# Moving a sum over 128 partitions from TensorE to GpSimd, and product P6 of one block behind P1 of the next

## The chip, the cores and the metric

One Trainium2 chip (trn2), one core. The metric is the device time of one execution in microseconds (us); a kernel is described by the median of its runs. Every run also has a profiled span, from the first recorded instruction to the last.

Names: TensorE (PE, its weight loads PEld), VectorE (DVE), ScalarE (ACT), GpSimd (POOL), SyncE (SP).

## The reference

```
x: (16, 256, 512), w1: (512, 4096), w2: (2048, 512), all float32
h = x @ w1
gate, value = split(h, 2)
h = maximum(gate, 0) * value
out = h @ w2
```

## The kernel before

The kernel works in float16 with float32 accumulation and replaces blocks of eight half-size products by seven products of sums (P1 to P7). Each of four stretches of 1024 rows goes through sixteen blocks of hidden columns (two plain ones at the very start) and then through the second matrix. Because sums in float16 can overflow or lose digits, squares of the inputs are collected in a tile `st` (128 x 152); at the end all entries must lie between two bounds. That is the verdict: VectorE counts the good entries of each partition, the 128 counts are added up, and a flag tells every engine whether to run a slow "general way", which is not taken here.

A block of seven products shares three PSUM tiles, X, Y and W, between TensorE (adds a product) and ScalarE or VectorE (reads what is there so far):

```python
def P1(self):                                   # TensorE -> X, then ScalarE copies X to Y
    self.X = psx.tile([P, TH], F32, name="X", tag="X")
    self.mm("P1", self.X, True)
    self.Y = psy.tile([P, TH], F32, name="Y", tag="Y")
    nc.scalar.copy(out=self.Y, in_=self.X)
def P5(self):                                   # TensorE -> W, ScalarE reads W into pu
    ...
    nc.scalar.activation(self.p5, self.W, COPY, scale=GS)
def P6(self):                                   # TensorE adds to Y, ScalarE reads Y into pu
    self.mm("P6", self.Y, False)
    nc.scalar.activation(self.u2, self.Y, COPY, scale=GS)
def P7(self):                                   # TensorE adds to Y again: only after that reading
    self.mm("P7", self.Y, False)
    nc.vector.scalar_tensor_tensor(out=self.c22, in0=self.Y, scalar=GS, in1=self.p5, op0=MULT, op1=ADD)
    ...
# ... cut: P2, P3, P4
```

P5, P6, P7 and P4 need weight sums T1 to T4, which GpSimd makes (`w_T<-w_stage`). Block 2 is the first of the seven-product kind, and its order is written by hand:

```python
for at, n in ((1, "P2"), (2, "P5"), (6, "P3")):
    plan[NPLAIN * PERIOD + at] = NPLAIN, n
plan[NPLAIN * PERIOD + 5] = NPLAIN + 1, "P1"
```

So TensorE runs P5, P6, P1 of block 3, P3, P5 of block 3, P7. The verdict at the end:

```python
def judge():                                    # VectorE: good entries of each partition
    # ... cut
    nc.vector.tensor_reduce(out=fit[:, :1], in_=ok, axis=mybir.AxisListType.X, op=ADD)
def count(fit):                                 # TensorE: sum over partitions, against a column of ones
    n = P * st.shape[1]
    ps = psx.tile([P, TH], F32, name="X", tag="X")
    nc.tensor.matmul(ps[:1, :1], fit[:, :1], fit[:, 1:], start=True, stop=True)
    nc.vector.tensor_scalar(out=flag, in0=ps[:1, :1], scalar1=n - 0.5, scalar2=None, op0=LT)
```

Of the kernel before, what the change touches and what calls it, by code (L numbers as in the profile page):

```python
# [9 lines left out]
F32, F32R, F16 = dt.float32, dt.float32r, dt.float16  # L10
ADD, SUB = mybir.AluOpType.add, mybir.AluOpType.subtract
MAX, MULT = mybir.AluOpType.max, mybir.AluOpType.mult
LE, GE, LT, ABS_MAX = (getattr(mybir.AluOpType, n) for n in ("is_le", "is_ge", "is_lt", "abs_max"))
# [3 lines left out]
P = 128  # L17
TH = 512
PERIOD = 7
NWARM = 24  # L20
NPLAIN = 2
# [5 lines left out]
@with_exitstack  # L27
def kernel(ctx: ExitStack, tc: tile.TileContext, x, w1, w2, out):






    nc = tc.nc
    x2 = x.flatten_outer_dims()
    out2 = out.flatten_outer_dims()
    flagpool = ctx.enter_context(tc.tile_pool(name="flagpool", bufs=1))
    flag = flagpool.tile([1, 1], dt.int32, name="flag")
    with ExitStack() as fast:  # L40
        unfit = fast_way(fast, tc, x2, w1, w2, out2, flag)
    with tc.If(unfit > 0, label="general"):
        with ExitStack() as general:
            general_way(general, tc, x2, w1, w2, out2)
# [52 lines left out]
def fast_way(ctx, tc, x2, w1, w2, out2, flag):  # L97
# [9 lines left out]
    nc = tc.nc  # L107
# [13 lines left out]
    wpool = ctx.enter_context(tc.tile_pool(name="wpool", bufs=1))  # L121
# [5 lines left out]
    psx = ctx.enter_context(tc.tile_pool(name="psx", bufs=3, space=bass.MemoryType.PSUM))  # L127
# [48 lines left out]
    def sums_of(o, eng=nc.vector):  # L176
        for n in SUMS_X:
            yield sum_of(o, n, eng)
# [257 lines left out]
    def advance(stream, n, todo={}):  # L436

        for _ in range(n):
            if stream is None:
                return  # L440
            at = stream_at[stream] = stream_at.get(stream, -1) + 1
            for job in todo.get(at, ()):
                job()
            next(stream, 0)
# [204 lines left out]
    def judge():  # L649
        n = st.shape[1]  # L650
        ok = wpool.tile([P, n], F32, name="ok")
        fit = wpool.tile([P, 2], F16, name="fit")
        nc.vector.tensor_scalar(out=ok, in0=st, scalar1=HIGH, scalar2=None, op0=LE)
        nc.vector.scalar_tensor_tensor(out=ok, in0=st, scalar=LOW, in1=ok, op0=GE, op1=MULT)
        nc.vector.memset(fit, 1.0)
        with nc.allow_low_precision("whole numbers below 2048"):
            nc.vector.tensor_reduce(out=fit[:, :1], in_=ok, axis=mybir.AxisListType.X, op=ADD)
        return fit

    def hint_here():  # L660
# [10 lines left out]

    def count(fit):
        n = P * st.shape[1]
        ps = psx.tile([P, TH], F32, name="X", tag="X")
        nc.tensor.matmul(ps[:1, :1], fit[:, :1], fit[:, 1:], start=True, stop=True)
        nc.vector.tensor_scalar(out=flag, in0=ps[:1, :1], scalar1=n - 0.5, scalar2=None, op0=LT)

    ats = [(1, jb) for jb in (0, 2, 4, 6, 8)] + [(2, jb) for jb in (0, 2, 4, 6, 8)] + [(3, jb) for jb in range(6)]
    for n, at in enumerate(ats):
# [11 lines left out]
    for s in range(NS):  # L691
# [5 lines left out]
        plan = {jb * PERIOD + at: (jb, n) for jb in blocks for n, at in SLOT.items()}  # L697
        if s == 0:
            for n in ("P5", "P2", "P3"):
                del plan[NPLAIN * PERIOD + SLOT[n]]  # L700
            del plan[(NPLAIN + 1) * PERIOD]
            for at, n in ((1, "P2"), (2, "P5"), (6, "P3")):
                plan[NPLAIN * PERIOD + at] = NPLAIN, n
            plan[NPLAIN * PERIOD + 5] = NPLAIN + 1, "P1"
        stream = None
        last = NJ * PERIOD
        todo = 3
        for at in range(first * PERIOD, (NJ - 1) * PERIOD + 14):
# [3 lines left out]
            if at in plan:  # L712
                jb, n = plan[at]
# [38 lines left out]
        def job(at, *what):  # L752
            jobs.setdefault(at, []).extend(what)
# [14 lines left out]
        if s + 1 < NS:  # L768
            xo = xo_next
            if s == 0:  # L770
                sums = sums_of(xo)
                for u in (84, 90):
                    job(u, lambda sums=sums: next(sums))
            looks = [lambda i=i: LOOK_JOBS[i]() for i in range(8 * s, 8 * s + 8)]
            advance(stream, 112 - TAIL - 10, jobs)
            if s == 0:
                next(sums)
                next(sums)
        else:
            verdict = []  # L780
            job(18, lambda: verdict.append(judge()))
            job(46, lambda: count(verdict[0]))
            job(78, lambda: verdict.append(nc.values_load(
                flag[0:1, 0:1], min_val=0, max_val=1, skip_runtime_bounds_check_because="a comparison wrote it")))
            job(40, hint_here)
            advance(stream, 112, jobs)
# [30 lines left out]
```

## Time and profile before

| | before |
|---|---|
| median time | 307.98 us at first (3 runs), 307.86 us with the three runs beside the changed kernel |
| span of the profiled run | 305.6 us (a run of 307.41 us, quicker than the six above) |
| TensorE busy | 300.7 us (98%) |
| chain that ended last | 96% TensorE |

From the page of the kernel before, part 1 (busy time of each engine) and part 4 (share of each engine in the chain that ended last):

```profile
PE 300.7 (98%) x1933; PEld 187.0 (61%) x1933; DVE 236.0 (77%) x388; ACT 176.5 (58%) x348; POOL 151.2 (49%) x189
PE 96%; DMA 1%; SPq 0%; POOL 0%; ACT 0%; issue 0%
```

Whatever is to gain must come out of TensorE's row. Where TensorE waited for another engine, by the list of waits of the kernel before (waiter, released by, us in total, times, longest):

```profile
PE Y L153 <- DVE warm L149: 1.2, 1, 1.2
PE W L332 <- POOL w_T L479: 0.2, 1, 0.2
```

Both are in the first 8 us. Shorter interruptions don't show there, so the timeline is needed. The start of the seven-product blocks in the kernel before (start, length, engine, line, operation, output and inputs, count, and in brackets the idle time before and who ended it):

```profile
15.60 0.69 DVE L174 TENSOR_TENSOR x_S<-x_A,x_S 128x1024 f16<-128x1024 f16 x1
15.64 1.24 POOL L237 TENSOR_TENSOR w_T<-w_stage 128x256 f16<-128x256 f32 x1 [2.51 <-DMA w_stage<-in_w_dram]
16.95 0.67 POOL L237 TENSOR_TENSOR w_T<-w_stage,w_T 128x256 f16<-128x256 f32 x1
17.05 0.60 PE L256 MATMUL W<-x_S,w_T 128*128 128x256 f16 x4
17.68 0.60 PE L256 MATMUL Y<-x_S,w_T 128*128 128x512 f16 x2
17.69 0.60 ACT L271 ACTIVATE pu<-W 128x512 f32<-128x512 f32 x1 [0.63 <-PE W L256]
18.12 0.59 PE L256 MATMUL X<-x_A,w_B 128*128 128x512 f16 x2
18.18 0.59 ACT L337 ACTIVATE v<-Y 128x512 f32<-128x512 f32 x1
18.66 0.60 ACT L278 ACTIVATE pu<-Y 128x512 f32<-128x512 f32 x1
19.14 0.62 ACT L264 COPY Y<-X 128x512 f32<-128x512 f32 x1
19.42 0.59 PE L256 MATMUL Y<-sq,w_T 128*128 128x512 f16 x2
```

Read it so. The matmul lengths overlap, so look at starts: a product takes 0.43 to 0.44 us. P5 (17.05) should be followed at 17.49, but P6 comes at 17.68, because its weight sum T2 (the GpSimd line at 16.95) ends at 17.62. P1 of block 3 is the X line at 18.12; P7 is the last line. The four ACT lines are a row without a gap: from 17.69 on, ScalarE starts something about every 0.48 us.

The other interruption is at the end of the stream (same view, kernel before):

```profile
286.90 0.60 PE L369 MATMUL Y<-v_T,w_stage 128*128 128x256 f16 x4
287.43 0.16 PE L675 MATMUL X<-fit 128*1 128x1 f16 x1
287.53 0.61 PE L369 MATMUL Y<-v_T,w_stage 128*128 128x256 f16 x4
287.98 1.04 PE L369 MATMUL W<-w,w_stage 128*128 128x256 f16 x8
```

Eight such matmuls take 0.87 us from start to start elsewhere; here it is 287.98 - 286.90 = 1.08 us, because the counting matmul stands in the middle.

### The profile page before, as it was taken

The page shows a single profiled execution, that of the slowest core. Times are in us where ns is not written, and L with a number is a line of the kernel's source. Part 1 is how long each engine was busy: PE and PEld are TensorE (multiplying, and loading weights), DVE is VectorE, ACT ScalarE, POOL GpSimd, SP SyncE. Part 2 cuts the span into 40 slices and gives each one's busy share as a digit, 9 for nine tenths or more (in the row PEclk, how much of TensorE's full clock was granted, in tenths as well). Part 3 has the DMA queues.
Part 4 walks back from the last instruction along what each step waited for, and adds up shares of the span by engine and source line. Part 5 has one row for each costly group of instructions (what it writes and reads, how often), then busy time and mean ns, then how long its engine had stood idle before and what let it go on. Part 6 is the DMA issues. An engine that isn't in the chain of part 4 may idle for free.

```text
span 305.6 us, 5338 instructions
## 1 busy us (share of the span) xinstructions
PE 300.7 (98%) x1933; PEld 187.0 (61%) x1933; DVE 236.0 (77%) x388; ACT 176.5 (58%) x348; POOL 151.2 (49%) x189
## 2 busy tenths in 40 slices
PE   8999999999999999999999999999999999999995
PEld 6854545688844444478864444458884444447884
DVE  2779888899768898887537888888546888888851
ACT  2588886455955555538855555545866555553231
POOL 2399999800069999300029989800006998800000
PEclk9999999999999999999999999999999999999999
DMA  7977679954794170001354910000325110000133
GB/s 236 356 233 219 213 176 177 223 114 87 266 200 92 64 138 3 0 2 63 136 175 108 206 36 2 0 2 2 138 91 185 35 34 2 1 1 27 45 105 107
DMA packets 35838, 32.89 MB, mean 108 GB/s; under 512 B 14432, under 2 KB 31328, under 8 KB 35680
## 3 DMA queue, kind: packets, MB, share of 16 engines
q1 hardware_dynamic: 33536, 26.22, 28.7%
q0 software_dynamic: 2272, 6.29, 11.6%
q8 instruction: 16, 0.26, 0.3%
q14 instruction: 14, 0.11, 0.1%
HBM read 27.26 MB, written 12.58 MB: 130 GB/s over the span
## 4 chain that ended last, share of the span: by engine, by line
PE 96%; DMA 1%; SPq 0%; POOL 0%; ACT 0%; issue 0%
PE Y L256 26%; PE W L256 18%; PE X L256 18%; PE Y L369 14%; PE X L369 9%; PE W L369 9%; DMA w_stage<-in_w_dram 1%; PE W L332 1%; PE X L332 1%; PE Y L332 1%; PE Y L511 0%; PE X L511 0%; SPq L501 0%; POOL w_T L479 0%; SPq L222 0%; ACT o L417 0%
## 5 line engine op out<-in xcount | busy, mean ns | idle before, releaser
L256 PEld LDWEIGHTS <-w_T 128*128 128x128 f16 x524 | 51.1, 98 | 54.6 <-POOL w_T L237 0.9
L184 POOL TENSOR_TENSOR fold<-xh 128x1024 f32<-128x1024 f16 x16 | 30.3, 1896 | 94.6 <-DMA xh<-x 93.7
L256 PE MATMUL X<-x_A,w_B 128*128 128x512 f16 x248 | 73.7, 379 | 0.0
L256 PE MATMUL Y<-x_S,w_T 128*128 128x512 f16 x220 | 65.4, 379 | 0.0
L256 PEld LDWEIGHTS <-w_B 128*128 128x128 f16 x372 | 36.4, 98 | 42.0
L284 DVE SCALAR_TENSOR_TENSOR cc<-W,pu 128x512 f32<-128x512 f32 x62 | 42.9, 692 | 21.3 <-ACT pu L278 21.3
L264 ACT COPY Y<-X 128x512 f32<-128x512 f32 x62 | 35.4, 571 | 38.2 <-PE X L256 37.9
L278 ACT ACTIVATE pu<-Y 128x512 f32<-128x512 f32 x62 | 37.1, 598 | 33.9 <-PE Y L256 32.9
L187 POOL TENSOR_TENSOR fold<-fold 128x512 f32<-128x512 f32 (+2 forms) x96 | 51.8, 540 | 7.5
L369 PEld LDWEIGHTS <-w_stage 128*128 128x128 f16 x512 | 50.0, 98 | 5.8
L294 DVE SCALAR_TENSOR_TENSOR cc<-Y,pu 128x512 f32<-128x512 f32 x62 | 42.9, 691 | 6.6
L289 DVE SCALAR_TENSOR_TENSOR g<-X,cc 128x512 f16<-128x512 f32 x62 | 42.9, 691 | 2.3
L306 DVE SCALAR_TENSOR_TENSOR g<-Y,cc 128x512 f16<-128x512 f32 x62 | 42.3, 682 | 1.8 <-PE Y L256 1.8
L369 PEld LDWEIGHTS <-g 128*128 128x128 f16 x384 | 37.5, 98 | 8.2
L271 ACT ACTIVATE pu<-W 128x512 f32<-128x512 f32 x62 | 37.2, 600 | 0.8 <-PE W L256 0.6
L256 PE MATMUL W<-x_S,w_T 128*128 128x512 f16 (+1 forms) x152 | 36.9, 340 | 0.0
L256 PE MATMUL W<-x_S,w_B 128*128 128x512 f16 x124 | 36.9, 379 | 0.0
L256 PE MATMUL Y<-x_A,w_T 128*128 128x512 f16 x124 | 36.9, 379 | 0.0
L369 PE MATMUL X<-w,g 128*128 128x256 f16 x256 | 31.9, 273 | 0.0
L405 DVE SCALAR_TENSOR_TENSOR o<-W,pu 128x256 f32<-128x256 f32 x16 | 6.8, 423 | 21.0 <-PE W L369 21.0
L174 DVE TENSOR_TENSOR w_stage<-g 128x1024 f16<-128x1024 f16 x32 | 21.4, 685 | 0.2
L237 POOL TENSOR_TENSOR w_T<-w_stage 128x512 f16<-128x512 f32 (+1 forms) x16 | 18.7, 1173 | 2.6 <-DMA w_stage<-in_w_dram 2.5
(100 smaller groups left out, 306.7 us busy)
## 6 DMA issues: line engine op xcount, KB each, us to landing
w_stage<-in_w_dram SPq DMA_DIRECT2D x14, 512.0 KB, 6.0
out_dram<-o SPq DMA_DIRECT2D x26, 256.0 KB, 2.2
x<-in_x_dram POOLq DMA_DIRECT2D x4, 1024.0 KB, 10.5
xh<-x SPq DMA_DIRECT2D x16, 256.0 KB, 3.2
w<-in_w_dram POOLq DMA_DIRECT2D x2, 1024.0 KB, 10.0
out_dram<-o SPq DMA_DIRECT2D x12, 128.0 KB, 1.7
w_stage<-in_w_dram SPq DMA_DIRECT2D x4, 256.0 KB, 4.8
x_S<-in_x_dram SPq DMA_DIRECT2D x4, 256.0 KB, 5.7
```

The source lines that it names most:

```text
L174: eng.tensor_tensor(o[n], o[i0], o[i1], op=op)
L184: nc.gpsimd.tensor_tensor(fold, t, t, op=MULT)
L187: nc.gpsimd.tensor_tensor(fold[:, :, :m], fold[:, :, :m], fold[:, :, m:2 * m], op=ADD)
L256: nc.tensor.matmul(ps[:, slice(*c)], wop[wn][:, b, self.jb * P:(self.jb + 1) * P], self.xo[xn][:, b, slice(*c)], start=fresh and b == c[0] ...
L264: nc.scalar.copy(out=self.Y, in_=self.X)
L271: nc.scalar.activation(self.p5, self.W, COPY, scale=GS)
L278: nc.scalar.activation(self.u2, self.Y, COPY, scale=GS)
L284: nc.vector.scalar_tensor_tensor(out=self.c12, in0=self.W, scalar=GS, in1=self.u2, op0=MULT, op1=ADD)
L289: nc.vector.scalar_tensor_tensor(out=self.g[:, self.jb, :TH], in0=self.X, scalar=0.0, in1=self.c12, op0=MAX, op1=MULT)
L294: nc.vector.scalar_tensor_tensor(out=self.c22, in0=self.Y, scalar=GS, in1=self.p5, op0=MULT, op1=ADD)
L306: nc.vector.scalar_tensor_tensor(out=self.g[:, self.jb, TH:], in0=self.Y, scalar=0.0, in1=self.c22, op0=MAX, op1=MULT)
L369: nc.tensor.matmul(ps, self.op[an][:, i], vop[wn][:, i], start=name in ("P1", "P5") and i == 0, stop=i == NJ // 2 - 1, skip_group_check=True)
```

## The change

The intent: fill the slot in which TensorE waits for T2 with a product that is ready (P1 of block 3), and take the counting matmul off TensorE by letting idle GpSimd add up the 128 counts. The diff:

```diff
     def judge():
-        fit = wpool.tile([P, 2], F16, name="fit")
+        fit = wpool.tile([P, 1], F32, name="fit")
         ...
-        nc.vector.memset(fit, 1.0)
-        with nc.allow_low_precision("whole numbers below 2048"):
-            nc.vector.tensor_reduce(out=fit[:, :1], in_=ok, axis=mybir.AxisListType.X, op=ADD)
+        nc.vector.tensor_reduce(out=fit, in_=ok, axis=mybir.AxisListType.X, op=ADD)
     def count(fit):
-        ps = psx.tile([P, TH], F32, name="X", tag="X")
-        nc.tensor.matmul(ps[:1, :1], fit[:, :1], fit[:, 1:], start=True, stop=True)
-        nc.vector.tensor_scalar(out=flag, in0=ps[:1, :1], scalar1=n - 0.5, scalar2=None, op0=LT)
+        total = wpool.tile([1, 1], F32, name="total")
+        nc.gpsimd.tensor_reduce(out=total, in_=fit, axis=mybir.AxisListType.C, op=ADD)
+        nc.gpsimd.tensor_scalar(out=flag, in0=total, scalar1=n - 0.5, scalar2=None, op0=LT)
     ...
-            for at, n in ((1, "P2"), (2, "P5"), (6, "P3")):
+            for at, n in ((1, "P2"), (2, "P5"), (5, "P6"), (6, "P3")):
                 plan[NPLAIN * PERIOD + at] = NPLAIN, n
-            plan[NPLAIN * PERIOD + 5] = NPLAIN + 1, "P1"
+            plan[NPLAIN * PERIOD + 4] = NPLAIN + 1, "P1"
     ...
-            job(46, lambda: count(verdict[0]))
+            job(18, lambda: count(verdict[0]))
```

## The prediction

> **What bounds the kernel now.** TensorE: the page gives it 300.7 of 305.6 us busy and 96% of the chain that ended last; granted clock 1.00. The list of waits shows two matmul waits, both before 8 us. After that matmuls run back to back (0.435 us for two 128x512, 0.87 us for eight 128x256). In the timeline the change touches two interruptions:
>
> 1. At 17.5 us P6 of block 2 waits for its weight sum T2 (GpSimd, 16.95 to 17.62). P5 would have freed TensorE at 17.49; P6 starts at 17.68: 0.19 us lost.
> 2. At 287.4 us the one-column counting matmul stands inside a product whose eight matmuls take 1.08 us instead of 0.87: 0.21 us lost.
>
> **What the change does.**
> (a) P1 of block 3 runs at 17.49; its weights and PSUM are ready, and T2 is ready for P6 at 17.92. This removes the 0.19 us. But it turns round two ScalarE instructions: block 3's copy Y<-X now precedes the reading of P6 (pu<-Y) of block 2. ScalarE is back to back there, about 0.48 us an instruction (before: pu<-W 17.69, v<-Y 18.18, pu<-Y 18.66 to 19.26, Y<-X 19.14 to 19.76). pu<-Y will end near 19.75, or 19.9, since the copy now waits for the end of v<-Y (same PSUM tile). P7 of block 2 writes the same Y and must wait for that reading. TensorE would reach P7 at 19.23 (19.42 before) and starts it at 19.8 to 19.95. A wait of 0.6 to 0.7 us replaces one of 0.19: net +0.4 to +0.5 us. Later TensorE has almost no wait to absorb it (0.04 us near 23 us), so it stays.
>
> (b) Removing the counting matmul gives back 0.21 us; the memset and the one-element VectorE comparison (0.06 and 0.14 us) are off the chain. GpSimd is idle there. The partition-axis reduction starts near 284.5 us and the flag is first loaded ten microseconds later, so up to about 9 us its own length is hidden. The risk is the port: the Trainium skill, "SBUF — State Buffer", says GpSimd and a VectorE operation with two SBUF inputs lock each other out for a whole instruction. This trace agrees: a 128x256 w_T sum that started at 15.64 beside VectorE's 128x1024 sum took 1.24 us instead of 0.67, ending 0.6 us after VectorE's. The VectorE sums due after the reduction (w_stage<-g, 0.68 us each) have about 2 us in hand: they end at 285.80 and 286.53, TensorE reads them at 287.98 and 288.85. A reduction that holds the port over 2 us would pass its excess to the end. "GPSIMD Engine Reference", section 3.2, gives 247.7 us for 2048 columns: an estimate of 0.12 us for one column plus a start of unknown size; no trace here shows it. I expect 0.5 to 2.5 us.
>
> **Sum.** +0.45 - 0.21 + about 0.2 (chance of port excess) = +0.4 us: 308.4 us, range 307.7 to 309.9. Faster by over 2%: 0.01; within 2%: 0.96; slower by over 2%: 0.03.
>
> **What would show it.** Right: no TensorE wait for GpSimd at 17.5 us, a new one of about 0.6 us for ScalarE's pu before P7 of block 2 (near 19.8 us), everything up to 280 us shifted later by 0.4 to 0.5 us; the product near 287 us back to 0.87 us. Wrong: P7 of block 2 at 19.3 us (then about 307.6), or w_stage sums near 285 us stretched by microseconds with TensorE waiting (309 or more).
>
> **What would make it wrong.** The reduction's length, and run-to-run spread (307.5 to 308.6), larger than the net effect.

## The result, and the profile after

| | before | after |
|---|---|---|
| median time (6 runs each) | 307.86 us | 308.48 us |
| lowest to highest | 307.52 to 308.58 | 308.30 to 309.32 |
| span of the profiled run | 305.6 us | 306.4 us |
| from P5 of block 2 to the last matmul (profiled runs) | 284.79 us | 285.05 us |

The ratio is 1.0019, with a 95% interval of 1.0002 to 1.0037: about 0.6 us slower, within 2%. A ratio is the mean time of one kernel's runs over that of the other's of the same rounds, so it is not quite the ratio of the medians.

Page and list of waits of the changed kernel:

```profile
PE 300.1 (98%) x1932; PEld 186.6 (61%) x1932; DVE 235.8 (77%) x386; ACT 176.7 (58%) x348; POOL 152.6 (50%) x191
PE 96%; DMA 2%; ACT 1%; SPq 0%; POOL 0%; issue 0%
PE Y L153 <- DVE warm L149: 1.2, 1, 1.2
PE W L332 <- POOL w_T L479: 1.0, 1, 1.0
PE Y L256 <- ACT pu L278: 0.6, 1, 0.6
```

ScalarE now has a share of the chain, and a matmul waits 0.6 us for ScalarE's `pu`. (By the starts, P7's wait is 0.71 us: 2.89 - 2.37 + 0.19, see below. The wait of L332 for GpSimd, 1.0 instead of 0.2 us, lies before 8 us. The start differs from run to run, as shown with the experiments: P5 of block 2 started at 17.52 us here and at 17.05 us in the profile of before.) The timeline of the same stage in the changed kernel:

```profile
17.42 0.67 POOL L237 TENSOR_TENSOR w_T<-w_stage,w_T 128x256 f16<-128x256 f32 x1
17.52 0.60 PE L256 MATMUL W<-x_S,w_T 128*128 128x256 f16 x4
17.96 0.59 PE L256 MATMUL X<-x_A,w_B 128*128 128x512 f16 x2
18.16 0.60 ACT L271 ACTIVATE pu<-W 128x512 f32<-128x512 f32 x1 [0.63 <-PE W L256]
18.39 0.59 PE L256 MATMUL Y<-x_S,w_T 128*128 128x512 f16 x2
18.66 0.59 ACT L337 ACTIVATE v<-Y 128x512 f32<-128x512 f32 x1
19.28 0.57 ACT L264 COPY Y<-X 128x512 f32<-128x512 f32 x1
19.76 0.60 ACT L278 ACTIVATE pu<-Y 128x512 f32<-128x512 f32 x1
20.41 0.59 PE L256 MATMUL Y<-sq,w_T 128*128 128x512 f16 x2 [0.56 <-ACT pu L278]
```

P5, P1 of block 3 and P6 now follow each other every 0.43 to 0.44 us: the slot is filled. But `Y<-X` now stands ahead of `pu<-Y`. It also starts only when `v<-Y` has ended (18.66 + 0.59 = 19.25, start 19.28), so `pu<-Y` ends at 20.36, and P7 waits for that. From P5 to P7 it was 19.42 - 17.05 = 2.37 us and is 20.41 - 17.52 = 2.89 us: 0.52 us lost.

The stage with the verdict, changed kernel:

```profile
285.33 0.68 DVE L174 TENSOR_TENSOR w_stage<-g 128x1024 f16<-128x1024 f16 x1
285.49 0.74 POOL L673 CROSS_LANE_REDUCE total<-fit 128x1 f32<-128x1 f32 x1 [17.69 <-DVE fit L655]
286.05 0.69 DVE L174 TENSOR_TENSOR w_stage<-w_stage,g 128x1024 f16<-128x1024 f16 x1
286.32 0.50 POOL L674 TENSOR_SCALAR flag<-total 1x1 int32<-1x1 f32 x1
287.84 1.04 PE L369 MATMUL Y<-v_T,w_stage 128*128 128x256 f16 x8
288.71 1.04 PE L369 MATMUL W<-w,w_stage 128*128 128x256 f16 x8
```

The product takes 288.71 - 287.84 = 0.87 us again. The reduction took 0.74 us, and VectorE's sums beside it kept their 0.68 and 0.69 us. (The first of them had started 0.16 us before the reduction; E7 shows a reduction that took 0.35 us.)

### The profile page after: what moved, and what is told of

Read it like the earlier page. It is cut to its first block, busy times and chain, and to the rows that moved or that the text cites. A ratio compares the mean times of both kernels' runs of the same rounds, so it can differ in the third digit from the quotient of the medians.

```text
span 306.4 us, 5336 instructions
## 1 busy us (share of the span) xinstructions
PE 300.1 (98%) x1932; PEld 186.6 (61%) x1932; DVE 235.8 (77%) x386; ACT 176.7 (58%) x348; POOL 152.6 (50%) x191
## 4 chain that ended last, share of the span: by engine, by line
PE 96%; DMA 2%; ACT 1%; SPq 0%; POOL 0%; issue 0%
PE Y L256 26%; PE X L256 17%; PE W L256 17%; PE Y L369 14%; PE X L369 9%; PE W L369 9%; DMA w_stage<-in_w_dram 2%; PE W L332 1%; PE X L332 1%; PE Y L332 1%; PE Y L511 0%; PE X L511 0%; SPq L501 0%; ACT v L337 0%; ACT Y L264 0%; POOL w_T L479 0%
```

## The experiments

All kernels gave a correct result. Two yardsticks besides the time are quieter than it. The first is the stretch from the start of P5 of block 2 to the start of the last matmul, taken from the traces: it is 284.77 to 284.79 us in five profiles of kernels that leave this part as before has it (before, E7, E9, E11, E12). A sixth, E8, gave 284.69 us; why is said there. What lies ahead of P5 hangs on the first loads and is not quiet: P5 started between 17.05 and 18.30 us in the profiles, and the spans of the kernel before ran from 305.4 to 306.5 us within the eleven runs of one batch. The second is the time above the span, the time of each run less its own span: 1.80 us on average in the kernel before in each of the first two batches of experiments (E1 to E4; E5, E7 to E9) and 1.85 in the third (E6, E10 to E12).

| kernel | median us | ratio to before (95%) | P5 to last matmul | time above span, mean |
|---|---|---|---|---|
| before | 307.86, 307.84, 308.05, 307.78 in four batches | 1 | 284.79 | 1.80 to 1.85 |
| after | 308.48 | 1.0019 (1.0002 to 1.0037) | 285.05 | 2.17 |
| E1 verdict only | 308.06 | 1.0018 (0.9999 to 1.0037) | 284.59 | 2.14 |
| E2 order only | 308.46 | 1.0021 (1.0008 to 1.0034) | 285.25 | 1.79 |
| E3 ScalarE's order restored | 308.11 | 1.0016 (1.0003 to 1.0028) | 284.49 | 2.16 |
| E4 one VectorE sum later | 307.90 | 1.0005 (0.9992 to 1.0018) | 284.71 | 1.78 |
| E5 no waits in the stage | 307.74 | 0.9992 (0.998 to 1.0005) | 284.66 | 1.83 |
| E6 E5, verdict by transfers | 311.64 | 1.0122 (1.0097 to 1.0146) | 286.80 | 2.01 |
| E7 unused GpSimd reduction | 308.00 | 0.9999 (0.9986 to 1.0012) | 284.78 | 1.95 |
| E8 reduction, never run | 307.77 | 0.9997 (0.9985 to 1.0009) | 284.69 | 1.97 |
| E9 flag on GpSimd | 307.95 | 0.9998 (0.9983 to 1.0012) | 284.79 | 1.97 |
| E10 19 columns (2 runs) | 310.27 | 1.0073 (1.0045 to 1.0102) | 286.77 | 2.17 |
| E11 eight memsets, never run | 307.98 | 1.0000 (0.9978 to 1.0023) | 284.77 | 1.84 |
| E12 general way's loads by SyncE | 310.45 | 1.0076 (1.0054 to 1.0099) | 284.78 | 1.78 |

My theory (A): the turned ScalarE order costs about 0.5 us, the verdict gives 0.2 us. Rival B: the verdict on GpSimd costs, the order is harmless. Rival C: it is start-up spread.

**E1: the verdict alone.** The diff above without its last two plan lines.

> Only the verdict on GpSimd, block order as before. Theory A (the turned ScalarE order costs, the verdict pays): about 0.2 us faster than before, ratio 0.9993, and no matmul wait near 19.6 us; the product near 287 us takes 0.87 us. Rival B (the verdict on GpSimd costs, by the port or the flag's path): slower than before by about 0.6 us, ratio 1.002. Rival C (nothing but start-up spread): ratio 1.000.

TensorE's stretch shrank by 0.20 us, as A said. The time did not follow: the median was 0.22 us above before (the ratio is pulled up by one run of 309.64). The ratio of 1.0018 is nearer to B's 1.002 than to A's 0.9993, though its interval includes C's 1.000 too; but B's mechanism was not met, as TensorE's stretch inside the span became shorter, not longer. What grew is the time above the span: 2.09 to 2.23 us in six runs, against 1.73 to 1.90 in the eleven runs of before beside them. Neither theory had that term.

**E2: the order alone.** The two plan lines, verdict as before.

> Only P1 of the next block ahead of P6, verdict as before. Theory A: about 0.5 us slower than before, ratio 1.0016 to 1.0018; P7 of block 2 waits 0.6 to 0.7 us for ScalarE's pu<-Y. Rival B: 0.2 us faster than before, ratio 0.9994. Rival C: ratio 1.000.

A held and B fell: ratio 1.0021, P7 waits for `pu<-Y`, from P5 (17.77) to P7 2.89 us, TensorE's stretch 0.46 us longer. P7 in this kernel:

```profile
20.66 0.59 PE L256 MATMUL Y<-sq,w_T 128*128 128x512 f16 x2 [0.56 <-ACT pu L278]
```

The missing 0.06 of the 0.52 us is a wait of before, 0.04 us near 23 us, that the delay swallows, and reading error.

**E3: TensorE's new order, ScalarE's old one.**

```diff
     def P1(self):
         ...
+        if not self.copy_later:
+            self.copy_X()
+    def copy_X(self):
         nc.scalar.copy(out=self.Y, in_=self.X)
     def P6(self):
         self.mm("P6", self.Y, False)
         nc.scalar.activation(self.u2, self.Y, COPY, scale=GS)
+        if self.then is not None:
+            self.then()
     ...                                          # cut: both attributes start as False and None
+            blocks[NPLAIN + 1].copy_later = True
+            blocks[NPLAIN].then = lambda: blocks[NPLAIN + 1].copy_X()
```

> The changed kernel, but block 3's copy Y<-X is issued on ScalarE behind block 2's pu<-Y, as it stood before; TensorE's order stays changed. Theory A: the wait of P7 falls from 0.6 us to about 0.1 us, both interruptions of TensorE are gone, and the time is about 0.3 us below before and 0.6 to 0.9 us below the changed kernel, ratio to before 0.999. Rivals B and C: as slow as the changed kernel, ratio 1.002 (B) or no clear difference to either (C).

The mechanism came out as A said. From the timeline of this kernel:

```profile
19.25 0.60 ACT L283 ACTIVATE pu<-Y 128x512 f32<-128x512 f32 x1
19.73 0.62 ACT L269 COPY Y<-X 128x512 f32<-128x512 f32 x1
19.91 0.59 PE L257 MATMUL Y<-sq,w_T 128*128 128x512 f16 x2
```

With the two ScalarE instructions back in their old order, `pu<-Y` ends at 19.85 and P7 follows at 19.91, 2.26 us after P5 (17.64) instead of 2.89. TensorE's stretch is 0.56 us shorter than in the changed kernel. The expected time was missed: 308.11 us, not below before, and 0.37 us below the changed kernel (another batch) where 0.6 to 0.9 was expected. By its ratio of 1.0016 alone it would speak for B; it is the trace that speaks for A. The term above the span (2.16 us) eats what the stretch gains; that the rest is start-up spread is not shown, as only one run of each kernel has a trace.

**E4: why T2 was late.** In the kernel before T1 took 1.24 us beside a VectorE sum with two SBUF inputs (15.60 above) and ended 0.59 us after it. The edit moves that sum:

```diff
-    sum_of(xo, "S4")
     held()
     ...
     plain[0].gate(1)
+    sum_of(xo, "S4")
```

> The kernel before with one edit: VectorE's sum S4 (128x1024, two SBUF inputs) stands behind the two gate operations instead of ahead of them, so that it no longer runs beside GpSimd's first weight sum T1. If T2 was late because the two engines exclude each other there: T1 takes about 0.67 us instead of 1.24, T2 ends near 17.0 instead of 17.62, P6's wait of 0.19 us is gone and the time is 0.2 us below before (ratio 0.9994). If T1 was slow by itself: it still takes 1.2 us and nothing moves.

```profile
16.52 1.28 DVE L341 SCALAR_TENSOR_TENSOR g<-X,v 128x512 f16<-128x512 f32 x2
16.53 0.73 POOL L237 TENSOR_TENSOR w_T<-w_stage 128x256 f16<-128x256 f32 x1 [2.50 <-DMA w_stage<-in_w_dram]
17.72 0.84 DVE L174 TENSOR_TENSOR x_S<-x_A,x_S 128x1024 f16<-128x1024 f16 x1
17.96 1.86 POOL L237 TENSOR_TENSOR w_T<-w_stage 128x256 f16<-128x256 f32 x2
```

Beside VectorE work with one operand in PSUM and one in SBUF, T1 took 0.73 us, and P6's wait was gone. The collision moved to where it harms nobody: the VectorE sum took 0.84 instead of 0.69 us and two GpSimd sums 1.86 instead of 1.42. So the mutual exclusion that the Trainium skill ("SBUF — State Buffer", section "SBUF: two separate sides") describes for GpSimd and two-input VectorE operations is what these runs show. The profile of E8 (below), in which nothing of this part was edited, shows the same the other way round. There GpSimd started 0.04 us before VectorE:

```profile
15.66 0.73 POOL L239 TENSOR_TENSOR w_T<-w_stage 128x256 f16<-128x256 f32 x1 [2.51 <-DMA w_stage<-in_w_dram]
15.70 1.23 DVE L176 TENSOR_TENSOR x_S<-x_A,x_S 128x1024 f16<-128x1024 f16 x1
```

Now VectorE's sum is the stretched one (1.23 us) and T1 takes 0.73 us. Of the eleven profiles with S4 in its old place, GpSimd was first in two (E3, E8: T1 0.83 and 0.73 us, S4 1.22 and 1.23). In the other nine S4 kept 0.68 to 0.69 us and T1 took 1.12 to 1.28 us; there S4 was first, but for E7, where the two starts lie 0.01 us apart.

In E4 the expected 0.2 us did not come: only 0.08 us of TensorE's stretch went, since P7 then waits 0.10 us for ScalarE and P2 0.06 us. A second limit stood close behind the first.

**E5: no wait in the stage at all.** E4, and the reading `v<-Y` moved from ScalarE to VectorE:

```diff
-        plain[1].value()
+        plain[1].value(on_vector=True)     # nc.vector.tensor_scalar(out=v, in0=W, scalar1=GS, op0=MULT)
```

> The kernel before with S4 behind the gate operations and the reading of the last plain product (v<-Y) moved from ScalarE to VectorE, which is idle there. If the stage near 17 to 21 us is bound by ScalarE's row of readings once T2 is early: neither P6, P7 nor P2 waits, and from the first P5 to the last matmul TensorE takes 284.55 us against 284.79 before and 284.70 with S4 moved alone; time about 0.2 us below before, ratio 0.9993 (near the spread). If not: P7 still waits 0.1 us and nothing is gained over S4 moved alone.

From P5 to P7 took 2.17 us, so P6 and P7 no longer wait, and neither does P2. Of the expected stretch (284.55 us) it reached 284.66: the wait for a GpSimd weight sum near 23.5 us grew from 0.04 to 0.11 us. In the list of waits of TensorE only the first remains:

```profile
PE Y L153 <- DVE warm L149: 1.2, 1, 1.2
```

The time was 307.74 us against 308.05, ratio 0.9992 with an interval that contains 1. It is the best kernel by its trace; that it is faster than before is not shown by its times.

**E7, E8, E9: what makes the time above the span.** E7 adds a GpSimd reduction over partitions, meant for 285 us, whose result is not used (its input was ready early, and it ran at 267.41 us); E8 puts one into the way not taken; E9 keeps the counting matmul and lets GpSimd compare and write the flag.

```diff
E7 +        nc.gpsimd.tensor_reduce(out=spare_total, in_=st[:, 24:25], axis=mybir.AxisListType.C, op=ADD)
E8 +    nc.gpsimd.tensor_reduce(out=spare_total, in_=ident[:, :1], axis=mybir.AxisListType.C, op=ADD)   # general_way
E9 +        nc.vector.tensor_copy(out=total, in_=ps[:1, :1])
E9 +        nc.gpsimd.tensor_scalar(out=flag, in0=total, scalar1=n - 0.5, scalar2=None, op0=LT)
```

> The kernel before with one GpSimd partition-axis reduction added near 285 us, whose result nothing reads; verdict by matmul as before. So far the time was above the profiled span by 1.79 us in the kernels with the counting matmul and by 2.15 us in the three with the GpSimd verdict. Theory D (an executed partition-axis reduction costs 0.36 us outside the span): difference 2.15 us, time about 0.36 us above before, span unchanged. Theory E (the comparison or the flag written by GpSimd costs it): difference 1.79 us, time as before.

> The kernel before with the partition-axis reduction only in the general way, whose branch is not taken, so that it is in the program and never runs. Theory D1 (its presence in the program costs, as something loaded or set up for it): difference of time and span 2.15 us. Theory D2 (running it costs, for instance at the end): 1.79 us. Theory E: 1.79 us.

> The kernel before, counting matmul kept, its result copied by VectorE and compared by GpSimd, which writes the flag. Theory E: difference of time and span 2.15 us, time 0.36 us above before. Theories D1 and D2: 1.79 us, time as before.

All three gave 1.95 to 1.97 us, between the two values, whether the added instruction was a reduction or a comparison and whether it ran or not. Theories D1, D2 and E fall in the form stated. Their times are not different from before. Two by-products: E7's reduction took half as long as the changed kernel's, with no two-SBUF-input sum of VectorE beside it, and E8 lost P6's wait (2.26 us from P5 to P7) because T1 won against S4 there, as shown under E4. P6's wait therefore depends on how a run starts: the 0.19 us that the change was to remove is not lost in every run. E7's reduction:

```profile
267.41 0.35 POOL L678 CROSS_LANE_REDUCE spare_total<-st 128x1 f32<-128x1 f32 x1
```

**E11 and E12: is it GpSimd's program length?** E11 adds eight memsets of GpSimd to the way not taken; E12 issues all transfers of that way from SyncE (`nc.gpsimd.dma_start` becomes `nc.sync.dma_start` in `general_way`).

> The kernel before with eight one-column memsets of GpSimd in the general way, which is not taken. One GpSimd instruction more raised the time above the span from 1.80 to 1.95 to 1.97 us, taken or not, and two (the changed verdict) to 2.15 us. If every further GpSimd instruction in the program costs that much: 3.0 to 3.2 us. If it is a matter of how the instructions fall in some pattern: between 1.7 and 2.3 us. Span as before.

> The kernel before with all transfers of the general way, which is not taken, issued by SyncE instead of GpSimd: GpSimd's program is some 80 instructions shorter, SyncE's as much longer, and nothing that runs is changed. If GpSimd's program length sets the time above the span: clearly below 1.80 us. If the total length of all programs does, or nothing of the kind: 1.80 us, or some other value if it is a matter of pattern.

Eight more GpSimd instructions gave 1.84 us, where the counting theory expected 3.0 us or more; it falls. A far shorter GpSimd program gave 1.78 us, against 1.85 for before in the same batch (1.76 to 1.91), so not clearly less. E12 was 2.7 us slower for other reasons that lie inside the span and were not followed up: its P5 started at 18.30 us, and from the last matmul to the end of the span it took 6.27 us instead of 3.80. So the 0.35 us above the span is measured (18 runs of three kernels with the changed verdict at 2.08 to 2.28 us, no run of before in the batches of experiments above 1.91), but its cause is open. It goes with the changed verdict's program, not with the number of GpSimd instructions.

**E10: a longer reduction.** 19 columns over the partitions instead of one, then a sum of the 19 on VectorE.

```diff
-        fit = wpool.tile([P, 1], F32, name="fit")
+        fit = wpool.tile([P, 19], F32, name="fit")
         ...                                      # cut: VectorE counts in 19 groups
-        nc.gpsimd.tensor_reduce(out=total, in_=fit, axis=mybir.AxisListType.C, op=ADD)
+        nc.gpsimd.tensor_reduce(out=parts, in_=fit, axis=mybir.AxisListType.C, op=ADD)
+        nc.vector.tensor_reduce(out=total, in_=parts, axis=mybir.AxisListType.X, op=ADD)
```

> The changed kernel, but GpSimd reduces 19 columns over the partitions instead of one. If the reduction grows by 0.12 us a column (from the skill's figure for 2048 columns) it takes near 2.9 us; if it holds the shared port for all of that, one VectorE sum w_stage<-g near 286 us ends some 2.2 us late and TensorE waits about 0.5 to 1 us near 288 us. If it doesn't hold the port: the sums keep 0.7 us each and TensorE doesn't wait. The result stays correct.

```profile
285.36 2.33 POOL L674 CROSS_LANE_REDUCE parts<-fit 128x19 f32<-128x19 f32 x1 [17.54 <-DVE fit L655]
287.72 0.16 DVE L675 TENSOR_REDUCE total<-parts 1x1 f32<-1x19 f32 x1 [2.45 <-POOL parts L674]
287.81 0.67 DVE L174 TENSOR_TENSOR w_stage<-g 128x1024 f16<-128x1024 f16 x1
288.54 1.05 PE L369 MATMUL W<-v_T,w_stage 128*128 128x256 f16 x8 [1.54 <-DVE w_stage L174]
```

TensorE did lose 1.5 us, but the experiment can't tell what I wanted to know: my added VectorE sum waits for the reduction and stands ahead of the next `w_stage` sum in VectorE's queue, so VectorE waited for a result and not for a port. Whether a reduction holds the port for all of its length stays open. What it shows is the length. VectorE was idle beside this reduction (2.45 us), so it is compared with E7's single column, which had no two-SBUF-input sum beside it either: (2.33 - 0.35) / 18 = 0.11 us a column.

**E6: neither TensorE nor GpSimd.** E5, and the 128 counts go to memory as a column and come back as a row; `count` also stands later in the stream (place 58 instead of 46):

```diff
+        nc.sync.dma_start(out=column, in_=fit)
+        nc.sync.dma_start(out=row, in_=column.rearrange("p o -> o p"))
-        nc.tensor.matmul(ps[:1, :1], fit[:, :1], fit[:, 1:], start=True, stop=True)
+        nc.vector.tensor_reduce(out=total, in_=fit, axis=mybir.AxisListType.X, op=ADD)
```

> S4 moved and v<-Y on VectorE as in the run before, and the verdict summed over partitions without TensorE and without GpSimd: the 128 sums go to memory and come back as one row by two small transfers, and VectorE adds them. Expected: the product near 287 us takes 0.87 us, from the first P5 to the last matmul 284.45 us (284.66 with the counting matmul), time above the span stays 1.8 us as no GpSimd instruction is added; about 0.4 us below before, ratio 0.9987. If a verdict off TensorE costs outside the span wherever it is done: difference of time and span near 2.15 us, time as before.

```profile
285.25 0.33 SPq L661 DMA_DIRECT2D column<-fit  x1
292.66 0.30 SPq L662 DMA_DIRECT2D row<-column  x1
296.11 0.28 DVE L680 TENSOR_REDUCE total<-row 1x1 f32<-1x128 f32 x1 [4.48 <-DMA row<-column]
297.29 0.60 PE L372 MATMUL X<-w,g 128*128 128x256 f16 x4 [2.05 <-DVE w_stage L174]
```

It failed by 3.9 us. The second transfer, which waits for the first, was issued 7.4 us after it and its row was read 3.45 us later. The sum's place in VectorE's queue came up long before that: VectorE waited 4.48 us for the row and TensorE 2.05 us for VectorE. Issued earlier or read later it might do; that was not tried. The time above the span was 2.01 us without any added GpSimd instruction.

## Why the prediction was right or wrong, point by point

- **Time.** 308.4 us was predicted, range 307.7 to 309.9; 308.48 us was measured, within 2% as expected.
- **P6's wait goes.** Right: P5, P1 and P6 run without a gap (17.52, 17.96, 18.39).
- **P7 waits for ScalarE instead.** Right in kind, a little too small: "+0.4 to +0.5 us" was 0.52 us from P5 to P7. (P7 came at 20.41 us and not at 19.8 to 19.95, because P5 itself started 0.47 us later in this profile.) The remark that the copy must also wait for `v<-Y` is what the trace shows. E2 gives the cost alone (0.46 us of the stretch), and E3, which restores ScalarE's order only, takes it away. That is the demonstration.
- **"0.04 us near 23 us".** Right: this wait of before is gone after.
- **The counting matmul gives back 0.21 us.** Right on TensorE: 0.20 us in E1.
- **The reduction and the port.** Expected 0.5 to 2.5 us, it took 0.74 us. The 0.2 us put into the sum for a port excess was not spent: the VectorE sums kept their length. The two engines did meet, but the other way round than feared: VectorE's sum had started 0.16 us earlier, and it was GpSimd's work that took longer than elsewhere (the reduction 0.74 us against 0.35 in E7, the comparison 0.50 us beside a VectorE sum against 0.23 in E9). That cost nothing, as TensorE loads the flag only at 293.3 us; the prediction's "first loaded ten microseconds later" holds for TensorE, while GpSimd itself loads it at 286.9 us.
- **What was missing.** The sum had no term for the time above the span. It rose by 0.33 to 0.37 us in the kernels with the changed verdict. Without it the sum is +0.52 - 0.06 - 0.20 = +0.26 us, which the stretch confirms (285.05 - 284.79); with it about +0.6 us, which the ratio confirms (1.0019, and 0.6 us between the two means). So the prediction's +0.4 us came close partly by luck: an allowance that was not needed stood in for a cost that was not known.
- **Verdict alone.** The belief that moving the verdict pays was wrong in its effect: inside the span it pays 0.2 us, but no gain in time is shown (E1).

## What to carry to other kernels

When a product is moved forward to fill a hole on the busiest engine, follow what it drags along on the engines that read its result: here the moved product's reader jumped the queue of a ScalarE row that had no gap, and a hole of 0.19 us became one of 0.71 us (2.89 - 2.37 + 0.19). A second limit can stand close behind the wait that one removes (E4: 0.19 us removed, 0.08 gained), so work out the next one before counting the gain. And compare the time with the span run by run: a cost that no view of the profile shows can be as large as the effect under study.

## What the Trainium skill lacked or had wrong

- "GPSIMD Engine Reference", section "Cross-partition — where GPSIMD wins", has one length for a reduction over partitions, 247,699 ns for 2048 columns (an estimate of 0.12 us a column). It lacks the small end: one column took 0.35 us (E7) and 0.74 us (the changed kernel, beside a VectorE sum with two SBUF inputs), 19 columns 2.33 us, so 0.11 us a column more, near that estimate.
- The same page, section "When to use GPSIMD", calls GpSimd the only option for a cross-partition reduce. A matmul against a column of ones did it here for 0.21 us of TensorE, and taking the sum to GpSimd instead gave no gain that is shown (E1: 1.0018, interval 0.9999 to 1.0037).
- "DMA: Bandwidth & Descriptors", section "Anatomy of one DMA — SWDGE (gpsimd) path", puts the fixed part of a transfer at about 2 us, for transfers of that path. What it lacks is a length for a case like E6's, which it doesn't contradict: the column of 128 single four-byte values, issued by SyncE, took 7.4 us from issue to landing and held its successor back for that long, while output transfers of 256 KB in the same trace took 2.1 us (median).
- No page has a time above the profiled span that changes with the program, as here: 1.8 us in the kernel before, 2.15 us with the changed verdict, cause open. The nearest is "Runtime: NRT & Kernel Launch", section "The launch sequence": it tells of a gap of about 6.2 us, much the same for every kernel measured there, by which the profile's total exceeds the reported time. Here the time exceeds the span, so it is not the same quantity.
